# Gates and branch products of a hybrid encoder with tokens on the partitions and 512 weight columns moving

## The chip, the core and the metric

The kernel runs on one core of one Trainium2 chip. The metric is the device time of one execution in microseconds. A profile is one execution recorded by the hardware profiler; its span runs from the first to the last instruction, and the time of that execution is a little longer than its span.

## The reference, cut to what matters

There are two layers, 256 tokens, a width of 1024 and fp32 throughout. A layer mixes the tokens in three ways beside each other (differential attention, a gated DeltaNet, windowed attention), each giving 512 channels. Each branch is multiplied by its own 512 x 1024 matrix and gated by a sigmoid of a projection of x; the three are summed and go through the output projection. A norm and an FFN follow.

```python
z = x @ w_in                                   # ... its last 3 * 1024 columns are gz
ys = jnp.stack([y_a, y_b, y_c], axis=2)        # 256 x 3 x 512
proj = jnp.einsum('btnc,ncd->btnd', ys, w_branch)
gates = jax.nn.sigmoid(gz.reshape(B, T, N_BRANCHES, D))
merged = jnp.sum(gates * proj, axis=2)
return merged @ w_out
```

## The kernel before

Nearly all of the work is fp32 products on TensorE. Each operand is held as a high half, rounded to the format in which TensorE is fast (`F32R`), and a low half, the rest; a product is three matmuls (`mm3`: high by high, high by low, low by high). Weights come in tiles of 128 x 1024 fp32, 512 KB each, packed on the host in the order of `_blocks`. `take` issues the load of a tile on SP's queue, copies it to the high half on ScalarE (`hi_take`) and subtracts to get the low half on VectorE (`lo_take`); there are 4 buffers each of the raw tile and of the two halves, and all weights form one stream in a fixed order.

There are two ways to lay out a projection. With channels on the partitions (`proj_ch`, and `pair` for two blocks of 128 channels in one PSUM bank) a 128 x 128 block of the weight is stationary and the 256 tokens of x^T (`xTh`, `xTl`) move. With tokens on the partitions (`token_major`, and `proj_tok` for the output projection `wo` and the FFN's way down `fd`) a slice of 128 tokens of x^T, or of the tile that holds the branch or FFN output, is stationary and 512 weight columns move.

`merge` returns `product`, which makes one product named in `ORDER`. A gate (`gz`, 12 a layer: 3 branches x 4 groups of 256 channels) is a `pair` followed by a tanh on ScalarE into a tile `g`; the sigmoid is (tanh + 1) / 2, and the half is applied at the end. A branch product (`wb`, 12 a layer) takes one weight tile and 24 matmuls of 256 tokens into one bank; then VectorE computes (g + 1) x product, and adds to the other branches' parts. After the third branch, ScalarE copies the sum, halved, to a high half and VectorE subtracts to get the low half (tiles `z` and `kk`, named `mh` and `ml`). They are then the stationary operand of the output projection, which needs channels on the partitions.

The order in which each engine works is written out before the kernel runs. Python records every operation (`Plan.record`; all of them carry line 195 in the profile), and `Plan.emit` walks through them as a list scheduler with estimated costs, ranks, and the offsets of `PRIO`. `ORDER` sets the order of the weight stream of the mixer's products. PSUM has 8 banks in three groups: 4 `mm` for the projections, 2 `ch` for the DeltaNet, 2 `at` for the attentions; the norm at the end of a part uses `ch` and `at` for its transposes. Gates and branch products that are ready fill TensorE while the mixers wait for other engines.

Of the kernel before, what the change touches and what calls it, by code (L numbers as in the profile page):

```python
# [10 lines left out]
F32 = mybir.dt.float32  # L11
F32R = mybir.dt.float32r
# [3 lines left out]
ALU = mybir.AluOpType  # L16
# [32 lines left out]
PRIO = {(0, 'a', 'ak', 0): -2.6, (0, 'a', 'aq', 1): 1.1, (0, 'a', 0): -0.1, (0, 'a', 1): 8.0, (0, 'a', 2): 6.9, (0, 'a', 3): -2.3, (0, 'ab', 0): -2.2, (0, 'aq', 0): -9.3, (0, 'aq', 1): -4.4, (0, 'c', 'ckv', 0): -20.4, (0, 'c', 'cq', 0): 5.9, (0, 'c', 0): -2.6, (0, 'c', 1): 2.1, (0, 'c', 2): -0.9, (0, 'cq', 0): 5.9, (0, 'cq', 1): 2.3, (0, 'finish'): -6.6, (0, 'gate', 1): 5.2, (0, 'gz', 0): -19.3, (0, 'gz', 1): -1.5, (0, 'gz', 3): -2.8, (0, 'k', 'ab', 0): -1.0, (0, 'k', 'gate', 0): -7.9, (0, 'k', 'gate', 1): 6.1, (0, 'k', 'q', 1): 2.4, (0, 'k', 'v', 0): -2.7, (0, 'k', 'v', 1): 7.3, (0, 'k', 0): -0.9, (0, 'k', 1): -10.1, (0, 'q', 0): 4.4, (0, 'q', 1): 8.0, (0, 'scan'): -3.1, (0, 'v', 0): -0.6, (0, 'v', 1): 4.5, (0, 'wb', 0): 5.9, (0, 'wb', 1): 4.2, (0, 'wb', 2): 4.8, (0, 'wb', 3): -13.0, (0, 'wb', 4): 7.1, (0, 'wb', 5): 4.3, (0, 'wb', 6): 7.1, (0, 'wb', 7): -4.2, (0, 'wb', 8): 0.1, (1, 'a', 'ak', 1): -4.1, (1, 'a', 'aq', 0): -0.2, (1, 'a', 'aq', 1): -4.3, (1, 'a', 0): 0.3, (1, 'a', 1): 3.1, (1, 'a', 3): -0.4, (1, 'ab', 0): -2.2, (1, 'ak', 0): 0.5, (1, 'ak', 1): 1.5, (1, 'aq', 1): 5.7, (1, 'av', 0): 5.4, (1, 'c', 'ckv', 0): 3.0, (1, 'c', 'cq', 0): -2.2, (1, 'c', 0): -3.8, (1, 'c', 1): 1.2, (1, 'ckv', 0): 3.0, (1, 'cq', 0): -1.5, (1, 'finish'): -4.0, (1, 'gate', 0): 7.5, (1, 'gate', 1): -5.5, (1, 'gz', 0): 3.8, (1, 'gz', 10): 4.4, (1, 'gz', 11): -5.4, (1, 'gz', 3): 8.2, (1, 'gz', 4): -3.2, (1, 'gz', 5): 0.4, (1, 'gz', 7): -3.0, (1, 'gz', 8): 14.3, (1, 'gz', 9): -2.7, (1, 'k', 'ab', 0): -3.5, (1, 'k', 'gate', 1): 1.4, (1, 'k', 'k', 0): -0.9, (1, 'k', 'q', 0): 3.4, (1, 'k', 'q', 1): 7.0, (1, 'k', 'v', 0): 3.3, (1, 'k', 'v', 1): 6.9, (1, 'k', 0): 5.2, (1, 'q', 0): 11.6, (1, 'q', 1): 1.6, (1, 'scan'): 0.7, (1, 'solve'): -7.1, (1, 'v', 0): 1.5, (1, 'v', 1): -1.0, (1, 'wb', 0): 8.7, (1, 'wb', 10): 2.6, (1, 'wb', 11): -3.3, (1, 'wb', 2): -2.3, (1, 'wb', 3): 3.1, (1, 'wb', 4): 4.9, (1, 'wb', 5): -1.6, (1, 'wb', 6): 2.9, (1, 'wb', 7): 9.9, (1, 'wb', 8): 3.9, (1, 'wb', 9): -0.1}  # L49
# [4 lines left out]
ORDER = [[('av', 0), ('ab', 0), ('k', 0), ('ak', 0), ('gz', 10), ('aq', 0), ('k', 1), ('q', 0), ('aq', 1), ('q', 1), ('ak', 1), ('gz', 1), ('v', 0), ('v', 1), ('gz', 0), ('gate', 0), ('gate', 1), ('cq', 0), ('wb', 1), ('ckv', 0), ('gz', 11), ('gz', 2), ('gz', 3), ('wb', 0), ('cq', 1), ('wb', 2), ('wb', 3), ('gz', 9), ('wb', 9), ('gz', 4), ('wb', 11), ('gz', 5), ('gz', 6), ('wb', 10), ('gz', 7), ('wb', 4), ('gz', 8), ('wb', 6), ('wb', 7), ('wb', 8), ('wb', 5)], [('av', 0), ('ab', 0), ('k', 0), ('ak', 0), ('gz', 10), ('aq', 0), ('k', 1), ('q', 0), ('aq', 1), ('q', 1), ('ak', 1), ('v', 1), ('gz', 0), ('gz', 3), ('v', 0), ('gate', 0), ('gate', 1), ('ckv', 0), ('gz', 1), ('cq', 0), ('wb', 1), ('wb', 0), ('gz', 11), ('gz', 2), ('cq', 1), ('wb', 2), ('gz', 9), ('wb', 3), ('gz', 4), ('wb', 9), ('wb', 11), ('gz', 5), ('gz', 6), ('wb', 10), ('wb', 4), ('gz', 8), ('gz', 7), ('wb', 6), ('wb', 7), ('wb', 8), ('wb', 5)]]  # L54


SIZES = {F32: 4, F32R: 4, F16: 2, U8: 1}
# [376 lines left out]
def _blocks(depth=DEPTH):  # L434

    out = []

    def cols(key, name, l, c0, n, nk=KD, k0=0, sub=()):
        out.append((key, nk, n, lambda i: i[name][(l,) + sub][k0 * P:(k0 + nk) * P, c0:c0 + n]))

    for l in range(depth):
        for nme, c, m in (("k", 2048, 4), ("q", 1536, 4), ("v", 2560, 4), ("gate", 3072, 4), ("aq", 0, 4), ("ak", 512, 4)):
            for b in range(m):
                cols((nme, l, b), "w_in", l, c + b * P, P)
        for b in range(4):
            cols(("av", l, b), "w_in", l, 1024, 512, 2, b * 2)
        for t in range(4):
            sel = np.concatenate([3600 + g * 256 + t * 64 + np.arange(64) for g in range(2)])
            out.append((("cq", l, t), KD, P, lambda i, l=l, sel=sel: i["w_in"][l][:, sel]))
        for b in range(2):  # L450
            cols(("ckv", l, b), "w_in", l, 4112 + b * P, P)
        for n in (0, 2, 1):
            for m in range(4):
                for b in range(2):
                    cols(("gz", l * 3 + n, 2 * m + b), "w_in", l, 4368 + n * D + (2 * m + b) * P, P)
                if n != 2:
                    cols(("wb", l, n, m), "w_branch", l, m * 256, 256, 4, sub=(n,))
                else:
                    sel = np.concatenate([g * 256 + t * 64 + np.arange(64) for t in range(4) for g in range(2)])
                    out.append((("wb", l, n, m), 4, 256, lambda i, l=l, m=m, sel=sel: i["w_branch"][l, 2][sel, m * 256:(m + 1) * 256]))  # L460
# [12 lines left out]
    return out  # L473
# [21 lines left out]
def tile_encoder_trunk(ctx: ExitStack, tc: tile.TileContext, a: dict, out: bass.AP, depth=DEPTH, tap=None):  # L495
# [191 lines left out]
    def pair(nme, l, b):  # L687
        return proj_ch([(nme, l, 2 * b + c) for c in range(2)])
# [691 lines left out]
    def merge(l, pr, ys, mh, ml):  # L1380
        gates, macc = {}, {}

        def product(nme, b):
            if nme == "av":
                return token_major(nme, l, "q")
            if nme == "ab":
# [8 lines left out]
                return ps  # L1395
            if nme == "gz":
                n, m = divmod(b, 4)
                ps = pair("gz", l * 3 + n, m)
                gates[b] = buf("g", (P, 2, T))
                S.activation(gates[b], ps, AF.Tanh, scale=0.5)  # L1400
                return None
            if nme != "wb":
                return pair(nme, l, b)
            n, m = divmod(b, 4)
            yh, yl = ys[n]
            gt = gates.pop(b)
            hi, lo = take(("wb", l, n, m))
# [20 lines left out]
    for l in range(depth):  # L1428
# [12 lines left out]
        tap(f"merged{l}", mh[0])  # L1441
# [64 lines left out]
```

## Time and profile before

| | |
|---|---|
| median of 3 executions | 993.6 us (992.38 to 994.38) |
| the profiled execution | 992.73 us |
| its span | 991.0 us |
| TensorE matmul busy | 969.0 us, 7598 instructions |
| VectorE, ScalarE, GpSimd busy | 722.3, 588.8, 73.0 us |
| read from HBM | 163.12 MB |

The page cuts the span into 40 equal slices and shows busy shares in tenths. The chain of work that ended last is followed back from the last instruction to what released each step. Busy times of matmuls overlap and their ends are modelled, so the spacing of matmuls is read from stretches of the chain.

### The profile page before, as it was taken

How to read it: one execution, taken by the hardware profiler on the slowest of the kernel's cores; microseconds unless marked ns; L12 is line 12 of the kernel's file. 1: busy time of each engine (PE TensorE's matmuls, PEld its weight loads, DVE VectorE, ACT ScalarE, POOL GpSimd, SP SyncE). 2: the span in 40 equal slices, each digit the busy share in tenths (PEclk: the TensorE clock that was granted, in tenths of full speed). 3: DMA queues.
4: the chain of work that ended last, by engine and by line, in shares of the span. 5: the costliest groups of instructions: out<-in, count | busy, mean ns of one | idle time of the engine just before them, and what ended most of it. 6: DMA issues, size and time to landing. Idle time of an engine off the chain costs nothing.

```text
span 991.0 us, 19154 instructions
## 1 busy us (share of the span) xinstructions
PE 969.0 (98%) x7598; PEld 906.2 (91%) x7598; DVE 722.3 (73%) x1310; ACT 588.8 (59%) x1068; POOL 73.0 (7%) x84
## 2 busy tenths in 40 slices
PE   7999999999999999999999999999999999999996
PEld 6899999989988999988889999999899799999885
DVE  6799786665689766665688996966756995667555
ACT  5868966664455655553557787757744654555441
POOL 0520010100000100000005200000000010000000
PEclk9999999999999999999999999999999999999998
DMA  7644355464575655555635543425445855555661
GB/s 266 187 153 147 102 148 145 144 182 138 178 248 168 203 187 186 172 175 188 213 104 158 165 121 115 146 81 176 154 137 181 273 190 159 191 180 188 196 191 42
DMA packets 50109, 165.43 MB, mean 167 GB/s; under 512 B 5751, under 2 KB 11271, under 8 KB 50020
## 3 DMA queue, kind: packets, MB, share of 16 engines
q1 hardware_dynamic: 48644, 159.78, 50.9%
q0 software_dynamic: 1376, 4.43, 1.5%
q8 instruction: 59, 0.97, 0.4%
q14 instruction: 30, 0.25, 0.1%
HBM read 163.12 MB, written 1.07 MB: 166 GB/s over the span
## 4 chain that ended last, share of the span: by engine, by line
PE 81%; DVE 6%; ACT 4%; DMA 2%; POOL 1%; issue 1%; POOLq 0%; DVEq 0%; ACTq 0%
PE mm_proj_ch L195 48%; PE ch_run L195 6%; PE mm_product L195 6%; PE mm_run L195 6%; PE mm_token_major L195 3%; PE at_window L195 2%; PE at_attention L195 2%; PE ch_solve L195 2%; DMA raw_proj_tok<-in_w_dram 2%; PE ch_gdn L195 1%; ACT hi_take L195 1%; PE ch_scan L195 1%; DMA raw_take<-in_w_dram 1%; PE ch_finish L195 1%; POOL x_decay L195 1%
## 5 line engine op out<-in xcount | busy, mean ns | idle before, releaser
L195 PE MATMUL mm_proj_ch<-xTh,hi_take 128*128 128x256 f32 x1488 | 421.8, 286 | 0.9 <-ACT hi_take L195 0.5
L195 PE MATMUL mm_proj_ch<-xTl,hi_take 128*128 128x256 f32 x1488 | 420.2, 285 | 0.0
L195 PE MATMUL mm_proj_ch<-xTh,lo_take 128*128 128x256 f32 x1488 | 419.1, 285 | 0.0
L195 DVE TENSOR_TENSOR lo_take<-raw_take,hi_take 128x1024 fp32r<-128x1024 f32 x219 | 266.8, 1232 | 104.5 <-ACT hi_take L195 86.4
L195 ACT ACTIVATE hi_take<-raw_take 128x1024 fp32r<-128x1024 f32 x214 | 224.4, 1057 | 195.0 <-PE mm_proj_ch L195 136.5
L195 PEld LDWEIGHTS mm_proj_ch<-xTh,hi_take 128*128 128x128 f32 x1488 | 280.2, 189 | 3.5 <-ACT hi_take L195 1.8
L195 PEld LDWEIGHTS mm_proj_ch<-xTh,lo_take 128*128 128x128 f32 x1488 | 279.5, 189 | 2.8 <-issue 1.6
L195 PEld LDWEIGHTS mm_proj_ch<-xTl,hi_take 128*128 128x128 f32 x1488 | 280.2, 189 | 1.6 <-issue 0.8
L195 ACT ACTIVATE hi_proj_tok<-raw_proj_tok 128x1024 fp32r<-128x1024 f32 x50 | 52.8, 1060 | 66.8 <-PE mm_run L195 37.9
L195 DVE TENSOR_TENSOR lo_proj_tok<-raw_proj_tok,hi_proj_tok 128x1024 fp32r<-128x1024 f32 x50 | 61.0, 1223 | 42.9 <-ACT hi_proj_tok L195 42.9
L195 DVE SCALAR_TENSOR_TENSOR z_conv_silu<-mm_proj_ch,col_params,z_conv_silu 128x254 f32<-128x254 f32 (+1 forms) x96 | 39.1, 474 | 0.6 <-ACT z_conv_silu L195 0.5
L195 DVE SCALAR_TENSOR_TENSOR g_product<-g_product,mm_product 128x512 f32<-128x512 f32 x24 | 16.5, 686 | 24.5 <-PE mm_product L195 24.5
L195 POOL TENSOR_TENSOR s_tail<-s_tail,nhalf 128x1 f32<-128x1 f32 x8 | 5.3, 665 | 380.4 <-DVE s_tail L195 380.4
L195 ACT ACTIVATE e_window<-e_window,s_window 128x256 f32<-128x256 f32 x55 | 26.5, 498 | 10.5 <-DVE s_window L195 10.4
L195 PEld LDWEIGHTS <-h_solve 128*128 128x128 f16 x640 | 25.8, 98 | 4.2 <-ACT h_solve L195 0.4
L195 PE MATMUL mm_run<-hi_proj_tok,tile_encoder_trunk 128*128 128x512 f32 x88 | 27.5, 392 | 1.6 <-ACT tile_encoder_trunk L195 1.2
L195 PE MATMUL mm_run<-hi_proj_tok,ile_encoder_trunk 128*128 128x512 f32 x88 | 27.3, 391 | 0.0
L195 ACT ACTIVATE e_attention<-e_attention,s_attention 128x256 f32<-128x256 f32 x46 | 22.7, 503 | 5.3 <-DVE s_attention L195 5.1
L195 PE MATMUL mm_product<-ya_attention,hi_take 128*128 128x256 f32 x128 | 25.1, 287 | 0.0
L195 PE MATMUL mm_product<-ya_gdn,hi_take 128*128 128x256 f32 x128 | 23.7, 283 | 0.0
L195 PE MATMUL mm_product<-yc_window,hi_take 128*128 128x256 f32 x128 | 23.7, 283 | 0.0
L195 ACT ACTIVATE tile_encoder_trunk<-tile_encoder_trunk 128x512 f32<-128x512 f32 (+1 forms) x22 | 13.6, 625 | 16.6 <-DVE tile_encoder_trunk L195 16.6
(348 smaller groups left out, 1656.0 us busy)
## 6 DMA issues: line engine op xcount, KB each, us to landing
raw_take<-in_w_dram SPq DMA_DIRECT2D x226, 512.0 KB, 4.2
raw_proj_tok<-in_w_dram SPq DMA_DIRECT2D x60, 512.0 KB, 4.0
G_load_G<-band SPq DMA_DIRECT2D x24, 192.0 KB, 3.5
ya_ln_params<-in_lnp_dram POOLq DMA_DIRECT2D x16, 256.0 KB, 5.9
x<-in_xT_dram SPq DMA_DIRECT2D x4, 256.0 KB, 4.5
x<-in_x_dram SPq DMA_DIRECT2D x2, 512.0 KB, 4.6
out_dram<-x SPq DMA_DIRECT2D x8, 128.0 KB, 1.8
_tile_encoder_trunk<-in_w_dram SPq DMA_DIRECT2D x4, 128.0 KB, 3.7
```

What stands on the lines that cost most here:

```text
L195: op.ways.append((eng, lambda fn=fn, args=args, kw=kw: fn(*args, **kw), _cost(eng, name, outs, ins, args, kw), table))
```

## The change

`product` no longer uses `pair` for the gates, nor 256 moving tokens for the branch products. Both are made 512 channels at a time: the slice of 128 tokens of x^T (gates) or of the branch's output (branch products) is stationary, and 512 columns of the weight move, into two PSUM banks, one for each half of the tokens. A gate is 4 weight tiles, a branch product is 2; there are 6 of each in a layer. Gating and summing are as before, on tiles with tokens on the partitions. The sum of the three branches is then turned over by four transposes on TensorE into a bank of the group `at`, and the copy to the high half and the subtraction read that bank. The output projection finds its stationary slices at the new places. `_blocks` packs the weights accordingly. `ORDER` and `PRIO` name the new products, and have other values for the rest too.

```diff
-ORDER = [[('av', 0), ('ab', 0), ('k', 0), ('ak', 0), ('gz', 10), ('aq', 0), ('k', 1), ('q', 0), ('aq', 1), ('q', 1), ('ak', 1), ('gz', 1), ('v', 0), ('v', 1), ('gz', 0), ('gate', 0), ('gate', 1), ('cq', 0), ('wb', 1), ('ckv', 0), ('gz', 11), ('gz', 2), ('gz', 3), ('wb', 0), ('cq', 1), ('wb', 2), ('wb', 3), ('gz', 9), ('wb', 9), ('gz', 4), ('wb', 11), ('gz', 5), ('gz', 6), ('wb', 10), ('gz', 7), ('wb', 4), ('gz', 8), ('wb', 6), ('wb', 7), ('wb', 8), ('wb', 5)],
...
+ORDER = [[('av', 0), ('ab', 0), ('k', 0), ('ak', 0), ('aq', 0), ('k', 1), ('gz', 0), ('q', 0), ('aq', 1), ('q', 1), ('ak', 1), ('v', 0), ('v', 1), ('gz', 1), ('gate', 0), ('gate', 1), ('cq', 0), ('ckv', 0), ('wb', 0), ('cq', 1), ('wb', 1), ('gz', 4), ('gz', 5), ('wb', 4), ('gz', 2), ('wb', 5), ('gz', 3), ('wb', 2), ('wb', 3)],
...
         for n in (0, 2, 1):
-            for m in range(4):
+            for h in range(2):
+                for b in range(KD // 2):
+                    cols(("gz", l * 3 + n, h, b), "w_in", l, 4368 + n * D + h * 512, 512, 2, b * 2)
                 for b in range(2):
-                    cols(("gz", l * 3 + n, 2 * m + b), "w_in", l, 4368 + n * D + (2 * m + b) * P, P)
-                if n != 2:
-                    cols(("wb", l, n, m), "w_branch", l, m * 256, 256, 4, sub=(n,))
...
+                    if n != 2:
+                        cols(("wb", l * 3 + n, h, b), "w_branch", l, h * 512, 512, 2, b * 2, sub=(n,))
...
+            if nme not in ("gz", "wb"):
+                return pair(nme, l, b)
+
+            n, h = divmod(b, 2)
+            nk = KD if nme == "gz" else 4
+            pss = [ps_mm() for _ in range(2)]
+            for c in range(nk // 2):
+                w = take((nme, l * 3 + n, h, c if nme == "gz" else 1 - c))
+                for tt in range(2):
+                    ts = slice(tt * P, (tt + 1) * P)
+                    for j in range(2):
+                        if nme == "gz":
+                            lh, ll = xTh[:, 2 * c + j, ts], xTl[:, 2 * c + j, ts]
+                        else:
+                            lh, ll = [y[1 - c][:, j, ts] for y in ys[n]]
+                        mm3(pss[tt], lh, ll, w[0][j], w[1][j], c == j == 0, 2 * c + j == nk - 1)
             if nme == "gz":
-                n, m = divmod(b, 4)
-                ps = pair("gz", l * 3 + n, m)
-                gates[b] = buf("g", (P, 2, T))
-                S.activation(gates[b], ps, AF.Tanh, scale=0.5)
+                gates[b] = [buf("g") for _ in range(2)]
+                for tt in range(2):
+                    S.activation(gates[b][tt], pss[tt], AF.Tanh, scale=0.5)
                 return None
...
-            ps = ps_mm((P, 2, T))
-            for c in range(2):
-                cs = slice(c * P, (c + 1) * P)
-                for j in (3, 2, 1, 0):
-                    mm3(ps[:, c], hi[j][:, cs], lo[j][:, cs], yh[j // 2][:, j % 2], yl[j // 2][:, j % 2], j == 3, j == 0)
-            V.scalar_tensor_tensor(gt, gt, 1.0, ps, ALU.add, ALU.mult)
-            parts = macc.setdefault(m, [])
-            parts.append(gt)
-            if len(parts) > 1:
-                V.tensor_tensor(parts[0], parts[0], gt, op=ALU.add)
-            if len(parts) == 3:
-                h_, l_ = [buf(("z", "kk")[m // 2], (P, 2, T), F32R) for _ in range(2)]
-                S.activation(h_, parts[0], AF.Copy, scale=0.5)
-                V.scalar_tensor_tensor(l_, parts[0], 0.5, h_.bitcast(F32), ALU.mult, ALU.subtract)
-                mh[m], ml[m] = h_, l_
+            for tt, gt in enumerate(gates.pop(b)):
+                V.scalar_tensor_tensor(gt, gt, 1.0, pss[tt], ALU.add, ALU.mult)
+                parts = macc.setdefault((h, tt), [])
+                parts.append(gt)
+                if len(parts) > 1:
+                    V.tensor_tensor(parts[0], parts[0], gt, op=ALU.add)
+                if len(parts) == 3:
+                    ps = ps_at((P, 4, P))
+                    for k in range(4):
+                        TE.transpose(ps[:, k], parts[0][:, k * P:(k + 1) * P], ident)
+                    h_, l_ = [buf(("z", "kk")[h], (P, 4, P), F32R) for _ in range(2)]
+                    S.activation(h_, ps, AF.Copy, scale=0.5)
+                    V.scalar_tensor_tensor(l_, ps, 0.5, h_.bitcast(F32), ALU.mult, ALU.subtract)
+                    mh[h, tt], ml[h, tt] = h_, l_
...
-        lhs = lambda k, tt: (mh[k // 2][:, k % 2, tt * P:(tt + 1) * P], ml[k // 2][:, k % 2, tt * P:(tt + 1) * P])
+        lhs = lambda k, tt: (mh[k // 4, tt][:, k % 4], ml[k // 4, tt][:, k % 4])
```

## Rows read from the trace of the kernel before

**Rows 1.** The page: busy time by engine, and busy tenths in 40 slices.
```profile
PE 969.0 (98%) x7598; PEld 906.2 (91%) x7598; DVE 722.3 (73%) x1310; ACT 588.8 (59%) x1068; POOL 73.0 (7%) x84
...
PE   7999999999999999999999999999999999999996
...
PEclk9999999999999999999999999999999999999998
```

**Rows 2.** Waits of TensorE (us in total, times, longest): first and last of 14.
```profile
PE mm_proj_ch L195 <- ACT _tile_encoder_trunk L195: 5.5, 1, 5.5
PE mm_run L195 <- ACT tile_encoder_trunk L195: 1.2, 1, 1.2
PE mm_token_major L195 <- DVE xTl L195: 0.9, 2, 0.5
...
PE mm_proj_ch L195 <- ACT q_token_major L195: 0.2, 1, 0.2
```

**Rows 3.** The chain in order of time: start us, us, what.
```profile
234.81 5.51 PE mm_product L195 x46
...
341.08 92.17 PE mm_proj_ch L195 x768
...
794.05 5.12 PE mm_token_major L195 x22
...
921.94 29.95 PE mm_run L195 x132
```

**Rows 4.** The chain at two runs of transposes; TensorE's timeline around four others.
```profile
201.16 0.87 PE ch_finish L195 x8
...
579.07 1.79 PE ch_gdn L195 x16
...
308.83 0.38 PE L195 MATMUL ch_tail<-tri,q_tail 128*128 128x128 f32 x2
309.05 0.38 PE L195 MATMUL at_tail<-tri,q_tail 128*128 128x128 f32 x2
309.19 0.48 PE L195 MATMUL mm_token_major<-yc_weights,xTh 128*128 128x512 f32 x1
309.50 0.39 PE L195 MATMUL mm_token_major<-yc_weights,xTl 128*128 128x512 f32 x1
```

**Rows 5.** Instructions on the tiles g and kk: ns min/median/max, first and last start.
```profile
L195 ACT ACTIVATE g_product<-mm_proj_ch x24: 573/579/609, 95.9 to 771.0; 128x512 f32<-128x512 f32 x24
L195 DVE SCALAR_TENSOR_TENSOR g_product<-g_product,mm_product x24: 681/686/689, 188.3 to 772.3; 128x512 f32<-128x512 f32 x24
L195 DVE TENSOR_TENSOR g_product<-g_product,g_product x16: 685/692/693, 239.3 to 773.0; 128x512 f32<-128x512 f32 x16
L195 ACT ACTIVATE kk_product<-g_product x4: 615/624/636, 267.5 to 774.0; 128x512 fp32r<-128x512 f32 x4
L195 DVE SCALAR_TENSOR_TENSOR kk_product<-g_product,kk_product x4: 684/686/693, 269.3 to 775.2; 128x512 fp32r<-128x512 f32 x4
```

**Rows 6.** DMA issues: count, KB each, median us to landing.
```profile
raw_take<-in_w_dram SPq DMA_DIRECT2D x226, 512.0 KB, 4.2
```

**Rows 7.** The chain in the windowed attention and at layer 0's handover.
```profile
212.25 1.08 ACT e_window L195 x5
...
274.27 0.70 DVE g_product L195
...
275.60 2.05 DVE lo_proj_tok L195 x2
...
279.19 1.22 DVE lo_proj_tok L195
...
283.38 7.56 DMA raw_proj_tok<-in_w_dram
```

**Rows 8.** VectorE's steps of the convolutions: ns min/median/max, first and last start.
```profile
L195 DVE SCALAR_TENSOR_TENSOR z_conv_silu<-mm_proj_ch,col_params,z_conv_silu x96: 465/474/484, 16.5 to 619.9; 128x254 f32<-128x254 f32 x48, 128x255 f32<-128x255 f32 x48
```

**Rows 9.** Busy us of PE, PEld, DVE, ACT, POOL in a stretch; clock; DMA share.
```profile
60.00:120.00 60.00, 59.50 (x697) 57.15 (x696) 53.28 (x112) 51.34 (x112) 6.39 (x7) 1.00 0.37 115
```

More of the change, by code (lines that the diff above doesn't have):

```diff
@@ L53 @@
 KEEP = {'wo': (4, ('D', 'N', 'x')), 'fd': ((4, ('g', 'g')), (4, ('g', 'g')))}
-ORDER = [[('av', 0), ('ab', 0), ('k', 0), ('ak', 0), ('gz', 10), ('aq', 0), ('k', 1), ('q', 0), ('aq', 1), ('q', 1), ('ak', 1), ('gz', 1), ('v', 0), ('v', 1), ('gz', 0), ('gate', 0), ('gate', 1), ('cq', 0), ('wb', 1), ('ckv', 0), ('gz', 11), ('gz', 2), ('gz', 3), ('wb', 0), ('cq', 1), ('wb', 2), ('wb', 3), ('gz', 9), ('wb', 9), ('gz', 4), ('wb', 11), ('gz', 5), ('gz', 6), ('wb', 10), ('gz', 7), ('wb', 4), ('gz', 8), ('wb', 6), ('wb', 7), ('wb', 8), ('wb', 5)], [('av', 0), ('ab', 0), ('k', 0), ('ak', 0), ('gz', 10), ('aq', 0), ('k', 1), ('q', 0), ('aq', 1), ('q', 1), ('ak', 1), ('v', 1), ('gz', 0), ('gz', 3), ('v', 0), ('gate', 0), ('gate', 1), ('ckv', 0), ('gz', 1), ('cq', 0), ('wb', 1), ('wb', 0), ('gz', 11), ('gz', 2), ('cq', 1), ('wb', 2), ('gz', 9), ('wb', 3), ('gz', 4), ('wb', 9), ('wb', 11), ('gz', 5), ('gz', 6), ('wb', 10), ('wb', 4), ('gz', 8), ('gz', 7), ('wb', 6), ('wb', 7), ('wb', 8), ('wb', 5)]]
+ORDER = [[('av', 0), ('ab', 0), ('k', 0), ('ak', 0), ('aq', 0), ('k', 1), ('gz', 0), ('q', 0), ('aq', 1), ('q', 1), ('ak', 1), ('v', 0), ('v', 1), ('gz', 1), ('gate', 0), ('gate', 1), ('cq', 0), ('ckv', 0), ('wb', 0), ('cq', 1), ('wb', 1), ('gz', 4), ('gz', 5), ('wb', 4), ('gz', 2), ('wb', 5), ('gz', 3), ('wb', 2), ('wb', 3)], [('av', 0), ('ab', 0), ('k', 0), ('ak', 0), ('aq', 0), ('k', 1), ('gz', 0), ('q', 0), ('aq', 1), ('q', 1), ('ak', 1), ('v', 0), ('v', 1), ('gz', 1), ('gate', 0), ('gate', 1), ('cq', 0), ('ckv', 0), ('wb', 0), ('cq', 1), ('wb', 1), ('gz', 4), ('gz', 5), ('wb', 4), ('gz', 2), ('wb', 5), ('gz', 3), ('wb', 2), ('wb', 3)]]
 SIZES = {F32: 4, F32R: 4, F16: 2, U8: 1}
@@ L452, in _blocks @@
         for n in (0, 2, 1):
-            for m in range(4):
+            for h in range(2):
+                for b in range(KD // 2):
+                    cols(("gz", l * 3 + n, h, b), "w_in", l, 4368 + n * D + h * 512, 512, 2, b * 2)
                 for b in range(2):
-                    cols(("gz", l * 3 + n, 2 * m + b), "w_in", l, 4368 + n * D + (2 * m + b) * P, P)
-                if n != 2:
-                    cols(("wb", l, n, m), "w_branch", l, m * 256, 256, 4, sub=(n,))
-                else:
-                    sel = np.concatenate([g * 256 + t * 64 + np.arange(64) for t in range(4) for g in range(2)])
-                    out.append((("wb", l, n, m), 4, 256, lambda i, l=l, m=m, sel=sel: i["w_branch"][l, 2][sel, m * 256:(m + 1) * 256]))
+                    if n != 2:
+                        cols(("wb", l * 3 + n, h, b), "w_branch", l, h * 512, 512, 2, b * 2, sub=(n,))
+                    else:
+                        sel = np.concatenate([g * 256 + t * 64 + np.arange(64) for t in (2 * b, 2 * b + 1) for g in range(2)])
+                        out.append((("wb", l * 3 + n, h, b), 2, 512, lambda i, l=l, h=h, sel=sel: i["w_branch"][l, 2][sel, h * 512:(h + 1) * 512]))
         for half in range(2):
@@ L1395, in product @@
                 return ps
+            if nme not in ("gz", "wb"):
[10 more added lines that the diff above has]
+                            lh, ll = xTh[:, 2 * c + j, ts], xTl[:, 2 * c + j, ts]
+                        else:
+                            lh, ll = [y[1 - c][:, j, ts] for y in ys[n]]
+                        mm3(pss[tt], lh, ll, w[0][j], w[1][j], c == j == 0, 2 * c + j == nk - 1)
@@ L1396, in product @@
             if nme == "gz":
-                n, m = divmod(b, 4)
-                ps = pair("gz", l * 3 + n, m)
-                gates[b] = buf("g", (P, 2, T))
-                S.activation(gates[b], ps, AF.Tanh, scale=0.5)
-                return None
[L1402 to L1407, printed above, removed]
-            ps = ps_mm((P, 2, T))
-            for c in range(2):
-                cs = slice(c * P, (c + 1) * P)
-                for j in (3, 2, 1, 0):
-                    mm3(ps[:, c], hi[j][:, cs], lo[j][:, cs], yh[j // 2][:, j % 2], yl[j // 2][:, j % 2], j == 3, j == 0)
@@ L1440, in tile_encoder_trunk @@
                 late.append((SY.dma_start(out=x[:, tt], in_=a["x"][0, tt * P:(tt + 1) * P]), 50 + 2 * tt))
-        tap(f"merged{l}", mh[0])
         norm = Norm(l, 1, pr["ln1_g"], pr["ln1_b"], False)
-        lhs = lambda k, tt: (mh[k // 2][:, k % 2, tt * P:(tt + 1) * P], ml[k // 2][:, k % 2, tt * P:(tt + 1) * P])
+        lhs = lambda k, tt: (mh[k // 4, tt][:, k % 4], ml[k // 4, tt][:, k % 4])
         proj_tok("wo", l, KD, lhs, norm)
```

2 lines of the change are left out of this document (1 added, 1 removed).

## The prediction

> **What bounds the kernel now.** I read the page's busy times first, then what TensorE waited for, then the chain of work that ended last in order of time, then the rows of the tiles that the diff touches. The reader is to see that TensorE is the bound nearly everywhere and that it is not slowed from outside: it is busy for 969.0 of 991.0 us, at a granted clock of 2.4 GHz, 0.9 or more of full speed, until the last slice [rows 1]. A busy TensorE is not a full one, since matmul ends are modelled, so the waits come next: in the whole span it stood with a named releaser for 11.8 us in 14 entries, 5.5 of them before the first matmul, and no entry names a PSUM bank that a reader had not yet emptied [rows 2]. So time that the change takes off TensorE should be nearly time off the end, and time that it adds to TensorE nearly time added.
>
> The price of a matmul is not the duration that the profile gives it, since matmuls overlap, but the spacing in a stretch where nothing else runs. The chain gives such stretches. With 256 moving columns: 768 in 92.17 us, 0.1200 us each, for x moving past stationary weights, and 46 in 5.51 us, 0.1198, for the branch products. With 512 moving columns there are two prices: 132 in 29.95 us, 0.2269, where the stationary operand is a slice of a mixer or FFN tile, and 22 in 5.12 us, 0.2327, where it is a slice of x^T [rows 3]. Two matmuls of 256 columns cost 0.240, so a matmul of 512 saves 0.013 or 0.007 us per pair. The gain per pair is small, and which price applies decides half of the gain.
>
> **The gates.** Before: 12 pairs a layer, each 2 blocks x 8 row blocks x 3 matmuls of 256 columns, so 576 a layer and 1152 in all: 1152 x 0.1200 = 138.2 us. After: 6 products a layer, each 4 weight tiles x 2 token halves x 2 x 3 matmuls of 512 columns, so 576 in all. Their stationary operand is xTh or xTl and their moving one is a weight tile, which is word for word the form of the token-major row: 576 x 0.2327 = 134.0, a gain of 4.2. By the other price 576 x 0.2269 = 130.7, a gain of 7.5. I take 4.2, because the operands are those of that row, and keep 7.5 as the other end.
>
> **The branch products.** Before 12 x 24 x 2 = 576 matmuls of 256: 576 x 0.1198 = 69.0 us. After 288 of 512 columns, stationary a slice of a mixer's output tile, so nearest to the 0.2269 row: 65.3, a gain of 3.7. By the dearer price 67.0, a gain of 2.0.
>
> **The turning over.** It is new: 4 transposes for each of 2 column halves x 2 token halves x 2 layers, 32 in all. Transposes in a row cost 0.87 us for 8 and 1.79 us for 16, so 0.109 to 0.112 each [rows 4]: 32 x 0.112 = 3.6 us. Beside that, a matmul of 512 columns that follows transposes starts its successor late: the one at 309.19 is followed after 0.31 us instead of 0.23 [rows 4]. Once for each of the 8 groups that is 0.6 us; nothing at the other end, if the planner puts groups together.
>
> **What is moved or stays equal.** The tanh (24 of 579 ns), the gating (24 of 686), the sums (16 of 692), the copies to the high half (8 of about 624) and the subtractions (8 of about 686) keep count and size, all 128x512 [rows 5]. The copy and the subtraction now read PSUM; ScalarE's 579 ns from PSUM against 624 from SBUF says that this is not dearer, and VectorE's 686 is the same from either [rows 5]. Weight tiles stay 72 of 512 KB over both layers, one copy and one subtraction each, on the same queue [rows 6]; a gate's tile now lasts TensorE 12 x 0.2327 = 2.8 us instead of 24 x 0.120 = 2.9, so no transfer has to be faster by more than a few per cent. No transfer is moved past another kind: the weights stay one stream on SP in a new order, and POOL's loads of the norm parameters still wait for the same freed tiles. What hides the equal work is TensorE's own stream; without that cover a group's sum, copy and subtraction cost 2.0 us.
>
> **The new waits.** First, a transpose waits for VectorE's sum, and behind it in TensorE's fixed order stand the output projection's matmuls. Before, the finished half went from VectorE to ScalarE directly. The handover already ran close: the chain leaves TensorE at 274.27 for VectorE's gating and the subtractions of the output weights, and then for a transfer of 7.56 us [rows 7]. TensorE had other matmuls meanwhile. After the last product the first column half needs no waiting, and its matmuls with two weight tiles and both token halves are 2 x 12 x 0.2269 = 5.4 us of cover; one group's path is 0.69 + 0.69 + 4 x 0.112 + 0.58 + 0.69 = 3.1 us, and the second group's VectorE work adds 2.1: 5.2 us. It just fits, so I cost it at nothing. Without the cover it is what stands in VectorE's queue ahead, two subtractions of weights of 1.2 us each [rows 7], 2.4 us a layer.
>
> Second, a gate holds two PSUM banks of four for 48 x 0.2327 = 11.2 us, where a pair held one for 48 x 0.120 = 5.8. Behind it in the first part of a layer stand the convolved projections, whose banks VectorE empties in 2 x 4 x 0.474 = 3.8 us each [rows 8], with VectorE at 53.28 of 60 us there [rows 9]. Two free banks and 11.2 us of gate matmuls to hide 3.8 us: at nothing, unless VectorE is more than 7.4 us behind.
>
> **The sum.** -4.2 - 3.7 + 3.6 + 0.6 = -3.7 us. The cheap ends give -7.5 - 3.7 + 3.6 = -7.6; the dear ends -4.2 - 2.0 + 4.2 = -2.0. The profiled execution took 992.73 us (span 991.0), so 989.0 by its own time; the median shown is 0.9 above it, so on that scale 989.9, with 986.0 to 991.6 as this case's own range.
>
> One rule speaks against the change. The Trainium skill, "TensorE: Matmul & The Clock Gate", section "Back-to-back issue gap", gives columns at one per cycle of 2.4 GHz and some 2.5 ns for each matmul. By that, 864 matmuls fewer are an estimate of 2.2 us, its 55.8 ns for 128 columns make 32 transposes 1.8 us, and the change would be worth under half a microsecond. The trace doesn't agree: the page's 109 ns for 256 columns stand here at 120, its 216 for 512 at 227 [rows 3].
>
> **The rivals.** (a) Not faster, because a gate's two banks starve the projections. For it: VectorE's load early in a layer [rows 9]. Against it: no bank wait among the 14 entries [rows 2]. Four gates stand among the convolutions (two a layer); if two of them leave TensorE waiting for one emptying of 3.8 us, +7.6: 997.5. It decides from one full emptying on, which eats the whole 3.7. (b) The handover takes the gain: 2.4 us in each of two layers, +4.9 on the sum, 994.8, within 991 to 997. For it: VectorE and the transfer are on the chain there [rows 7]. Against: the cover computed above. (c) No gain per column: a matmul of 512 columns costs two of 256 when its moving operand is a fresh weight tile; then only the turning over is left, +4.2, 997.8. The token-major row, which moves fresh weights, speaks against it at 0.2327 against 0.240. (d) More than the sum: all at 0.2269, and the new order, which puts 5.4 us of branch product and two gates of 11.2 us between the last projection of the windowed attention and its product, fills the stretch in which its softmax on ScalarE and VectorE is on the chain from 212.25 [rows 7]; about 2 us a layer more than -7.6 would give 982 to 986, taken as 984.
>
> **How the numbers follow.** Chances: the sum 0.57, (a) 0.13, (b) 0.17, (c) 0.04, (d) 0.09. A difference of 0.2% is 2.0 us, about what a measurement of this kernel can tell from none. Faster: 0.51 from the sum and all of (d), 0.60. Same: 0.06 from the sum, 0.12 from (b) and 0.01 from (a), 0.19. Slower: 0.21, the rest. The predicted time is the sum's, 989.9. From 984 to 999 the range leaves out half of (d) and somewhat over half of (a), about 0.12, with the rest of the 0.2 for what I didn't think of.
>
> **What would show it.** Right: the gate's matmuls spaced 0.232 to 0.233 us, the branch products' 0.227, 32 transposes at 0.11, TensorE's waits still near 12 us. (a) would show as waits of projections for VectorE's convolutions or as wide spacing right behind a gate; (b) as a wait of transposes or of the output projection on VectorE near 275 and 765 us; (c) as spacing of 0.240; (d) as both forms at 0.227 and a mixer stage shorter by more than its matmuls. The prediction is wrong if TensorE's gaps between products, which the list of waits hardly shows, change by more than 4 us with the new order.

## The result and the profile after

| | before | after |
|---|---|---|
| median | 993.87 us (992.38 to 994.38) | 985.95 us (985.11 to 986.52) |
| ratio | | 0.9924, interval 0.9911 to 0.9938 |
| profiled execution, its span | 992.73, 991.0 us | 986.52, 984.8 us |
| TensorE instructions | 7598 | 6766 |

The kernel became faster by 7.9 us by the medians, 6.2 by the spans of the two profiles. The forecast was 3.7 us faster; the time lies inside the range of 984 to 999, just below the sum's own range of 986.0 to 991.6.

The page of the changed kernel: busy time by engine and busy tenths, to be held against [rows 1].

```profile
PE 960.6 (98%) x6766; PEld 859.9 (87%) x6766; DVE 724.2 (74%) x1313; ACT 586.9 (60%) x1065; POOL 72.5 (7%) x84
...
PE   7999999999999999999999999999999999999996
...
PEclk9999999999999999999999999999999999999999
```

TensorE is busy 8.4 us less and still bounds the kernel. What it waited for (us in total, times, longest), to be held against [rows 2]: four of the first eight, and the last, of 15.

```profile
PE mm_proj_ch L195 <- ACT _tile_encoder_trunk L195: 5.1, 2, 4.9
PE ch_tail L195 <- DVE q_tail L195: 1.5, 1, 1.5
PE mm_run L195 <- ACT ile_encoder_trunk L195: 1.2, 1, 1.2
...
PE mm_product L195 <- DVE z_conv_silu L195: 0.5, 1, 0.5
...
PE at_window L195 <- DVE yc_window L195: 0.2, 1, 0.2
```

All 15 come to 14.4 us, 2.6 more than before. None is a transpose of the sum, and none an output projection (`mm_run`) that waits for `z` or `kk`; the `mm_run` here belongs to the FFN's way down, as in [rows 2]. One is a PSUM bank of the projections: at 540.45 a gate's matmul, which doesn't read `z_conv_silu`, starts right behind the last convolution step with which VectorE reads a bank. Read in the same way, `at_window` behind `yc_window` is a bank of the group `at`, and so is the last entry of [rows 2] one of the group `mm`: a matmul behind the ScalarE copy that empties a bank. All of these are short, 0.2 to 0.5 us.

The chain of the changed kernel in order of time, at the long products of both layers and a windowed softmax ahead of those of layer 1, their handover to the output projection in layer 0, and the start of the FFN and of the way down; to be held against [rows 3] and [rows 7].

```profile
208.78 62.52 PE mm_product L195 x269
271.30 0.44 PE at_product L195 x4
271.74 1.39 PE mm_product L195 x6
273.13 0.44 PE at_product L195 x4
273.56 5.50 PE mm_product L195 x24
279.06 1.82 PE mm_run L195 x8
280.87 0.44 PE at_product L195 x4
281.31 1.40 PE mm_run L195 x6
...
339.70 91.86 PE mm_proj_ch L195 x768
...
435.26 29.31 PE mm_run L195 x128
...
704.08 1.26 ACT e_window L195 x5
...
713.71 44.02 PE mm_product L195 x190
...
916.43 29.32 PE mm_run L195 x128
```

The gates, mixed with some branch products, are spaced 62.52 / 269 = 0.2324 and 44.02 / 190 = 0.2317; the last branch product is spaced 5.50 / 24 = 0.229. From 271 to 282 the chain passes through the transposes and never leaves TensorE. Before, it ran there over VectorE and a transfer of 7.56 us [rows 7].

TensorE's timeline around two groups of transposes in layer 1:

```profile
757.57 0.60 PE L195 MATMUL at_product<-tri,g_product 128*128 128x128 f32 x4
757.93 0.48 PE L195 MATMUL mm_product<-hi_take,ya_gdn 128*128 128x512 f32 x1
758.24 0.60 PE L195 MATMUL at_product<-tri,g_product 128*128 128x128 f32 x4
758.60 0.48 PE L195 MATMUL mm_product<-hi_take,ya_gdn 128*128 128x512 f32 x1
758.91 0.40 PE L195 MATMUL mm_product<-lo_take,ya_gdn 128*128 128x512 f32 x1
```

Four transposes take 0.36 us, and the matmul behind them is followed after 0.31 us instead of 0.23: 0.36 + 0.08 = 0.44. That is the chain's 0.44 for a group, so the slowed step behind the group was already in the chain's 0.11 for each transpose [rows 4], and the forecast's extra 0.6 us counted it twice.

The other engines' instructions on the changed tiles (ns minimum, median, maximum; first and last start), to be held against [rows 5]:

```profile
L195 ACT ACTIVATE g_product<-mm_product x24: 572/598/667, 135.0 to 750.5; 128x512 f32<-128x512 f32 x24
...
L195 DVE SCALAR_TENSOR_TENSOR g_product<-g_product,mm_product x24: 679/681/689, 199.2 to 762.4; 128x512 f32<-128x512 f32 x24
...
L195 ACT ACTIVATE kk_product<-at_product x4: 578/599/601, 281.4 to 767.6; 128x512 fp32r<-128x512 f32 x4
```

They kept count and size, as forecast, and the copies of the sum to the high half, now from PSUM, take 596 (`z`) and 599 ns (`kk`) by the median where those from SBUF took 624.

**Where the 6.2 us went.** TensorE's timeline can be cut into steps from each matmul's start to the next one's, and the steps summed by product; idle time then counts to the product ahead of it. The gates of before carry the same name as other channel projections; they are taken as what those projections shrink by, 576 matmuls a layer, as if the others had not changed.

| us of TensorE's timeline | before | after | difference | forecast |
|---|---|---|---|---|
| gates and branch products, layer 0 | 109.2 | 106.2 | -3.0 | -3.95 |
| gates and branch products, layer 1 | 110.1 | 104.2 | -5.9 | -3.95 |
| transposes | 0 | 2.8 | +2.8 | +4.2 |
| all else (from the span) | | | -0.1 | 0 |
| span | 991.0 | 984.8 | -6.2 | -3.7 |

The prices come from the chain of the kernel before, at its own gates and branch products in layer 0, and, for comparison, at the FFN of layer 1:

```profile
257.10 4.63 PE mm_proj_ch L195 x39
...
263.03 2.63 PE mm_product L195 x22
...
893.21 28.30 PE mm_proj_ch L195 x238
```

A gate's matmul of 256 columns was spaced 4.63 / 39 = 0.1187 us (0.1188 over all gates from 237 to 275 us), not the 0.1200 of the FFN's long stretch in layer 0 [rows 3]; the FFN of layer 1 has 0.1189. A branch product's was 2.63 / 22 = 0.1195. After the change the two are 0.2324 and 0.229. So the gates' matmuls gained 1152 x 0.1188 - 576 x 0.2324 = 3.0 us and the branch products' 576 x 0.1195 - 288 x 0.229 = 2.9.

At these prices a layer's gates and branch products would take 102.8 us before and 99.9 after. The rest, 6.4 and 7.3 us before, 6.3 and 4.3 after, is time beyond the prices; it hardly moved in layer 0 and fell by 3.0 in layer 1. Not all of it is TensorE standing still. Of the 864 matmuls in the changed kernel's products, 67 come right behind a matmul of another kind (transposes, attention, DeltaNet) and have a step that is 0.04 to 0.12 us longer, like the 0.31 above; together these are 5.8 of the 10.6 us. The end of the way down's long run of matmuls, a mark that nothing overtakes, agrees: 466.3 before and 464.6 after in layer 0, 951.9 and 945.8 in layer 1, so 1.7 us came from layer 0 and 4.4 from layer 1.

### The profile page after: what moved, and what is told of

Same layout as the page of the kernel before. It is cut to its first block, busy times and chain, and to the rows that moved or that the text cites. A ratio compares the mean times of both kernels' runs of the same rounds, so it can differ in the third digit from the quotient of the medians.

```text
span 984.8 us, 17469 instructions
## 1 busy us (share of the span) xinstructions
PE 960.6 (98%) x6766; PEld 859.9 (87%) x6766; DVE 724.2 (74%) x1313; ACT 586.9 (60%) x1065; POOL 72.5 (7%) x84
## 4 chain that ended last, share of the span: by engine, by line
PE 83%; ACT 7%; DVE 6%; DMA 1%; issue 1%; POOL 1%; SPq 0%; POOLq 0%; ACTq 0%; DVEq 0%
PE mm_proj_ch L195 37%; PE mm_product L195 17%; PE mm_run L195 8%; PE ch_run L195 8%; PE mm_token_major L195 4%; PE ch_solve L195 2%; PE at_attention L195 2%; ACT e_window L195 2%; ACT hi_take L195 1%; DVE lo_take L195 1%; PE at_window L195 1%; DVE z_conv_silu L195 1%; PE ch_gdn L195 1%; POOL D_decay L195 1%; ACT s_window L195 1%
## 5 line engine op out<-in xcount | busy, mean ns | idle before, releaser
L195 PE MATMUL mm_proj_ch<-xTh,hi_take 128*128 128x256 f32 x1104 | 310.6, 285 | 0.7 <-ACT hi_take L195 0.6
L195 PE MATMUL mm_proj_ch<-xTh,lo_take 128*128 128x256 f32 x1104 | 309.7, 284 | 0.0
L195 PE MATMUL mm_proj_ch<-xTl,hi_take 128*128 128x256 f32 x1104 | 309.4, 283 | 0.0
L195 PEld LDWEIGHTS mm_proj_ch<-xTh,hi_take 128*128 128x128 f32 x1104 | 207.6, 189 | 2.4 <-ACT hi_take L195 0.8
L195 PEld LDWEIGHTS mm_proj_ch<-xTl,hi_take 128*128 128x128 f32 x1104 | 207.8, 189 | 0.7 <-DVE xTl L195 0.2
L195 PEld LDWEIGHTS mm_proj_ch<-xTh,lo_take 128*128 128x128 f32 x1104 | 207.3, 189 | 1.0 <-DVE lo_take L195 0.4
L195 PE MATMUL mm_product<-hi_take,xTh 128*128 128x512 f32 x192 | 76.7, 406 | 1.0 <-DVE z_conv_silu L195 0.5
L195 PE MATMUL mm_product<-lo_take,xTh 128*128 128x512 f32 x192 | 76.9, 402 | 0.1
L195 PE MATMUL mm_product<-hi_take,xTl 128*128 128x512 f32 x192 | 76.4, 399 | 0.0
L195 PEld LDWEIGHTS mm_product<-lo_take,xTh 128*128 128x128 f32 x192 | 36.3, 189 | 7.8 <-DVE lo_take L195 0.8
```

What stands on the lines that cost most here:

```text
L195: op.ways.append((eng, lambda fn=fn, args=args, kw=kw: fn(*args, **kw), _cost(eng, name, outs, ins, args, kw), table))
```

## The experiments

The first theory was that the two layout terms (-7.9) come through whole and that the transposes cost nothing, since they stand in a handover where TensorE waits anyway. Its rival was that the layout is worth the forecast's 3.7 us and the rest is the new order of work. e1, e2 and e4 to e6 change what is issued with the order of work held; e3 and e7 to e12 change the order. Changes against the changed kernel are differences of medians to 985.95; e1 to e4, e5 to e8 and e9 to e12 had the kernel before beside them at 992.47, 992.71 and 992.78 us. The diffs are shortened to what they do.

**e1: the moving operand halved again.** 768 of the 864 gate and branch matmuls are issued as two of 256 columns.

```diff
-mm3(pss[tt], lh, ll, w[0][j], w[1][j], c == j == 0, 2 * c + j == nk - 1)
+# each of mm3's matmuls but those with start or stop:
+for c0 in (0, 256):
+    nc.tensor.matmul(ps[:, c0:c0 + 256], lx, rx[:, c0:c0 + 256], start=start, stop=stop)
```

> The changed kernel with the same order on every engine, but 768 of the 864 gate and branch matmuls are issued as two of 256 moving columns (the first and the last of each bank stay whole). Theory P (the price per column is what the layout gains): 528 gate matmuls cost 0.240 instead of 0.2324 and 240 branch matmuls 0.239 instead of 0.2267, so +4.0 + 3.0 = +7.0 us on the changed kernel, about 993. Theory L (the layout gains by something else, and the moving width is not the cause): within 1 us of the changed kernel, about 986.

Measured 989.12 us (987.29 to 991.88), ratio 0.9969 [0.9958, 0.998]: 3.2 us slower than the changed kernel. In TensorE's timeline the products took 215.0 us instead of 210.3, so the halving cost 4.6 us there, less than twice the 0.1200 of [rows 3] would have made (7.0) and near what twice 0.1188 and 0.1195 makes (528 x 0.0052 + 240 x 0.010 = 5.1); 3.2 of them reached the end. The gain from 512 columns is real, and a matmul of 512 does not cost two of 256.

**e2: no turning over.** The transposes are left out; the copy and the subtraction read the sum as it is, so the output projection gets operands with rows and columns exchanged.

```diff
-TE.transpose(ps[:, k], parts[0][:, k * P:(k + 1) * P], ident)
+# nothing is issued in its place
-S.activation(h_, ps, AF.Copy, scale=0.5)
+S.activation(h_, parts[0], AF.Copy, scale=0.5)
```

> The changed kernel with the same order, without the 32 transposes: the copy and the subtraction read the sum before it is turned over, so the output projection multiplies a wrong operand and only the turning over is left out. Theory P: every transpose is on TensorE's path, -3.6 - 0.6 = -4.2 us on the changed kernel, about 981.8. Theory L (TensorE has slack there, the handover is bound by VectorE or by transfers): 0 to -1 us.

Measured 988.1 us (985.32 to 989.35), ratio 0.9948 [0.9933, 0.9963]: no faster than with the transposes. Two stretches at half the clock lie in its profile, of which more below; at 1.6 us each, as an estimate, its span without them would be 984.5, against 984.8. In layer 0 the last product's last matmul does start earlier, at 277.1 instead of 278.7, but the output projection's last one only 0.7 us earlier. The chain of this kernel shows why:

```profile
274.25 1.23 DVE lo_proj_tok L195
...
275.49 7.54 DMA raw_proj_tok<-in_w_dram
...
283.60 1.05 ACT hi_proj_tok L195
```

With TensorE's transposes gone, the transfer of the output projection's weights sets the handover again, as before the change [rows 7]; in layer 1 too, with 5.25 us. By these two profiles taking 3.5 us of transposes out is worth 0.3 us. Two profiles of equal work differ by more (982.3 us in e4), so what is shown is that no gain near 3.5 us came.

**e5 and e6: work added with the order held.** e5 issues every transpose twice; e6, the control, issues the first matmul of each of the 24 gate groups twice.

```diff
 # e5
-TE.transpose(ps[:, k], parts[0][:, k * P:(k + 1) * P], ident)
+plan.record(("PE", "transpose", twice(nc.tensor.transpose), (ps[:, k], parts[0][:, k * P:(k + 1) * P], ident), {}))
 # e6
+if nme == "gz" and c == j == 0:
+    plan.record(("PE", "matmul", twice(nc.tensor.matmul), (pss[tt], lh, w[0][j]), {"start": True, "stop": False}))
...
```

> The changed kernel with each of the 32 transposes issued twice, in the same order of work; the output stays the same. If the transposes stand in stretches in which TensorE waits for VectorE or for weights anyway (hidden), 32 more cost 0 to 1 us against the changed kernel, ratio to the kernel before 0.992 to 0.9935. If they stand on the work that sets the end (paid), 32 x 0.09 to 0.112 = 2.9 to 3.6 us more, ratio 0.9953 to 0.996.

> The control: the changed kernel with the first of the 24 matmuls of each of the 24 gate groups issued twice (the first time into a closed group, so the output stays the same), in the same order of work: 24 x 0.2325 = 5.6 us of TensorE's time in the gates. If TensorE sets the time in the stretches with gates, 4 to 5.6 us more than the changed kernel, ratio to the kernel before 0.9965 to 0.998. If the mixer stage has slack that takes up such additions, as the halved matmuls let suppose, 0 to 3 us more, ratio 0.9924 to 0.9955.

e5 measured 988.52 us (986.7 to 990.47), ratio 0.9948 [0.9931, 0.9966]: 2.6 us slower for 32 x 0.108 = 3.5 us more on TensorE. e6 measured 989.8 us (988.24 to 991.4), ratio 0.9965 [0.9951, 0.9978]: 3.9 us slower for 5.6. So about 0.7 of what is added to TensorE reaches the end, in the gates and in the transposes alike. The share depends on what is taken as the changed kernel's time: by the ratios to the kernel before beside each, e1, e5 and e6 are 4.5, 2.4 and 4.1 us slower, which is between 0.7 and all of what was added. That is against the first theory: the transposes are not free, they are just at the edge, where the handover is as long by TensorE as by the transfer. Less of them gains nothing that shows, more of them costs.

**e3: the kernel before in the new order.** ORDER and PRIO of the changed kernel, each product of 512 channels written as its two of 256.

```diff
-ORDER = [[('av', 0), ('ab', 0), ('k', 0), ('ak', 0), ('gz', 10), ('aq', 0), ('k', 1), ('q', 0),
+ORDER = [[('av', 0), ('ab', 0), ('k', 0), ('ak', 0), ('aq', 0), ('k', 1), ('gz', 0), ('gz', 1), ('q', 0),
...
```

> The kernel before, layout untouched, with the changed kernel's order of weights and planner offsets (each product of 512 channels replaced by its two products of 256 in a row, with its offset). Theory P (layout gives -3.7, the other 4 of the -7.9 come from the new order and offsets): 989 to 991. Theory L (all of it comes from the layout): 993 to 996, the old time or worse, since the offsets were made for other products.

Measured 1001.64 us (1000.19 to 1003.17), ratio 1.009 [1.0076, 1.0104]: slower by 9.2 us. The new order by itself gives the old layout nothing; it was made for the other one, which is 15.7 us faster in it. The reverse, the changed kernel in the order of before, was not run.

**e7 to e12: three pairs of the two layouts under other offsets.** In each kernel PRIO alone is changed: emptied, halved, or layer 1 given the values of layer 0.

```diff
+PRIO = {}                                          # e7 after, e8 before
+PRIO = {k: v / 2 for k, v in PRIO.items()}         # e9 after, e10 before
+PRIO = {(l,) + k[1:]: v for l in (0, 1) for k, v in PRIO.items() if k[0] == 0}   # e11 after, e12 before
```

> The changed kernel with the table of offsets PRIO emptied; ORDER stays. To be read against e8, the kernel before with its table emptied. If the gain comes from the layout alone (gates -4.2, branch products -3.7, transposes hidden), this one is 7 to 8 us faster than e8. If the layout is worth the 3.7 us of the forecast and the tuned offsets the rest, 3 to 4 us faster than e8. Both are expected slower than with their tables, by 5 to 30 us.

> The kernel before with the table of offsets PRIO emptied; ORDER stays. Layout alone: 7 to 8 us slower than e7. Layout 3.7 and offsets the rest: 3 to 4 us slower than e7. Whatever the difference is beyond 8 us would be the planner's luck with either order.

> The changed kernel with every offset of PRIO halved; ORDER stays. To be read against e10, the kernel before with its offsets halved. With all offsets (profiles) the layout with its own order gained 1.7 us in the mixer of layer 0 and 6.1 in that of layer 1; with none, e7 was 2.8 us faster than e8. If the layout by itself is worth 7 us and more, this one is 6 to 9 us faster than e10, and both layers gain alike. If the layout is worth the 3 to 4 us of its matmuls and transposes, and the rest is stalls of TensorE that one order has and another has not, the pair differs by 0 to 6 us, and the two layers differ from each other by several us, not in the same way as in the tuned pair.

> The kernel before with every offset of PRIO halved; ORDER stays. Layout worth 7 us by itself: 6 to 9 us slower than e9. Layout worth 3 to 4 us and the rest the order's stalls: 0 to 6 us slower than e9. Both are expected above their tuned kernels, by 5 to 25 us.

> The changed kernel with layer 1 given the offsets of layer 0 (ORDER is the same for both of its layers already). Layer 0 should stay as it was, output projection ending near 296 us. If the layout by itself gains 6 us in layer 1's mixer, it ends that mixer 5 to 7 us sooner than e12 by stage length. If those 6 us are the order's, the stage lengths of layer 1 differ by another amount, 0 to 4 us or with the other sign.

> The kernel before with layer 1 given the offsets of layer 0; the two ORDER lists stay. Layer 0 as before, output projection ending near 298 us. Layout worth 6 us in layer 1: its mixer stage takes 5 to 7 us longer than in e11. The order's: another difference, 0 to 4 us or with the other sign.

| offsets | before's layout | new layout | difference | layer 0, layer 1 (profiles) |
|---|---|---|---|---|
| tuned | 993.87 | 985.95 | -7.9 | -1.7, -4.4 |
| none (e8, e7) | 1018.85 | 1016.04 | -2.8 | -4.0, +2.1 |
| halved (e10, e9) | 1016.93 | 1002.0 | -14.9 | -10.8, -4.2 |
| layer 0's in both (e12, e11) | 1011.23 | 997.45 | -13.8 | -2.2, -13.0 |

The last column is the mark at the end of the way down's long run. Their ratios to the kernel before: e7 1.0226 [1.0207, 1.0245], e8 1.0256 [1.0235, 1.0277], e9 1.0087 [1.0074, 1.0101], e10 1.0246 [1.0232, 1.0261], e11 1.0042 [1.0026, 1.0057], e12 1.0189 [1.0172, 1.0205]. The new layout is faster in all four pairs, but by 2.8 to 14.9 us, and layer by layer between 13.0 us faster and 2.1 slower, where the operations are the same and only their order differs. Layer 0 of the last pair has the offsets of the tuned kernels and repeats their difference (-2.2 against -1.7), so this scatter belongs to the orders and not to the measurement.

By the estimate below, most of the scatter is the clock. In e7 to e12 TensorE's granted clock falls from 2.4 to 1.2 GHz for a while, behind places where the order has left it thinly used. Here are, for e7 and then for e8, the 3 us ahead of such a stretch at the handover of layer 0, and all stretches at half the clock. Columns: stretch; its length, busy us (count) of PE, PEld, DVE, ACT, POOL; granted clock, DMA share, GB/s.

```profile
190.50:197.30 6.80, 5.95 (x16) 4.40 (x17) 4.28 (x21) 5.39 (x18) 0.00 (x0) 0.50 0.27 57
...
286.50:289.50 3.00, 1.22 (x4) 0.59 (x4) 3.00 (x5) 2.07 (x5) 0.10 (x1) 1.00 0.92 298
289.50:296.30 6.80, 5.81 (x18) 4.86 (x19) 5.99 (x10) 4.62 (x9) 0.00 (x0) 0.50 0.90 299
...
685.40:695.60 10.20, 7.36 (x30) 6.00 (x30) 6.16 (x32) 7.84 (x25) 1.67 (x2) 0.50 0.22 56
...
791.30:794.70 3.40, 3.40 (x12) 2.71 (x11) 2.96 (x5) 2.55 (x5) 0.00 (x0) 0.51 0.90 301
```

```profile
74.00:77.40 3.40, 3.31 (x29) 3.13 (x30) 3.35 (x6) 3.24 (x5) 0.00 (x0) 0.50 0.62 202
...
217.40:220.80 3.40, 3.40 (x15) 2.26 (x16) 0.98 (x4) 1.47 (x4) 0.00 (x0) 0.50 0.00 0
...
292.90:295.90 3.00, 1.20 (x4) 0.67 (x4) 3.00 (x5) 3.00 (x6) 0.53 (x1) 1.00 0.98 300
295.90:299.30 3.40, 3.10 (x7) 2.48 (x8) 2.05 (x4) 0.03 (x1) 0.00 (x0) 0.50 0.94 306
...
794.20:797.60 3.40, 3.40 (x10) 2.64 (x9) 1.28 (x3) 0.00 (x0) 0.00 (x0) 0.51 0.99 383
```

The tuned kernels have no such stretch before their last matmuls. On the way down one of 3.4 us cost 1.6 us (see the last section), so half of the length is an estimate of what a stretch costs, on the high side where TensorE also stands within it.

| offsets | us at half the clock, before's layout | new layout | difference of the spans | less the clock's part, an estimate |
|---|---|---|---|---|
| tuned | 0 | 0 | -6.2 | -6.2 |
| none | 13.7 | 27.3 | -2.0 | -8.8 |
| halved | 17.1 | 3.4 | -15.0 | -8.2 |
| layer 0's in both | 17.1 | 6.8 | -15.2 | -10.1 |

All executions of these kernels bear it out: the mean granted clock is 0.984 in e7 and 0.989 to 0.993 in e8, 0.993 to 0.996 in e9 and 0.986 to 0.989 in e10. Without the clock's part the new layout gains 6 to 10 us in every pair, and in each layer of every pair (1.7 to 7.9). By the prices above and 0.44 us for each of the 8 groups it would be -3.0 - 2.9 + 3.5 = -2.4, in any order. What goes beyond, some 4 us in the tuned pair and 6 to 8 in the others, is time beyond the prices, which the new layout had less of each time; 0.6 to 0.9 us of it lies ahead of the first matmul. Neither theory as written holds: the layout's own price is not 7 us, and the pairs differ by more than 0 to 6, by way of the clock.

Without offsets, the handover that the forecast feared does come. What TensorE waited for in e7:

```profile
PE mm_run L195 <- DVE z_product L195: 4.3, 2, 2.2
...
PE mm_run L195 <- ACT z_product L195: 1.5, 2, 0.8
```

and in e8, the kernel before without offsets:

```profile
PE mm_run L195 <- DVE z_product L195: 3.3, 2, 1.6
PE mm_run L195 <- ACT z_product L195: 3.2, 2, 1.6
```

There all eight transposes of the first column half follow the last product in a row, and TensorE stands 5.8 us, over both layers, for the output projection's operands. But the layout of before stands 6.5 us at the same place, so it is no price of the turning over alone. In both kernels the clock falls right behind it (289.5 and 791.3 in e7, 295.9 and 794.2 in e8).

**e4: the address of x^T.** 96 bytes are allocated ahead of `xTh`, to see whether its place is why a matmul with x^T stationary costs more than one with a mixer's tile.

```diff
+cp.tile([P, 24], F32, name="pad")
 xTh = cp.tile([P, KD, T], F32R, name="xTh")
```

> The changed kernel with 96 bytes in front of the x^T tiles, so that they and everything behind them start elsewhere (x^T at a multiple of 4096 bytes, the rest at a multiple of 64). If the gate's dearer price of 0.2324 against 0.2267 hangs on where x^T lies: gates at about 0.227, -3.3 us for the gates and -1.1 for the token-major projections, about 981.5. If it hangs on something else of these operands: 0.2324 as before and about 986.

Measured 985.15 us (983.98 to 986.24), ratio 0.9924 [0.9911, 0.9937], with the gates still spaced 62.55 / 269 = 0.2325. The address is not the cause. As the computation is unchanged, this is also a second measurement of the change: 7.3 us against its own runs of the kernel before.

## Why the prediction was right, and where its size was off

- **The bound.** Right: of time added to TensorE 0.7 or more reaches the end (e1, e5, e6).
- **The gates, -4.2, and the branch products, -3.7: right in kind, too large.** The price for 512 columns holds in the gates, 0.2317 to 0.2324 against the 0.2327 assumed. The one for 256 was taken from the FFN's 768 matmuls at 0.1200, while the gates of before were spaced 0.1187, so the term is -3.0. The branch products came to 0.229 instead of 0.2269, so theirs is -2.9. In the timeline the two terms make -8.9 us, 3.0 more than these prices, all of it less time beyond the prices in layer 1.
- **The turning over, +3.6 and +0.6: counted twice in part.** Each group cost 0.44 us, as priced, but the 0.6 for the matmul behind a group was in that price already. In the timeline the transposes took 2.8 us and the slowed steps behind them the rest, within the products. With this and the terms above the forecast's own sum is -3.0 - 2.9 + 3.5 = -2.4 us, smaller than it stated. And leaving the transposes out gave no gain that shows (e2), because the transfer of the output weights takes the handover over.
- **The new waits, at nothing.** Right for the handover: the first two groups are turned over before the last product ends, the other two lie under matmuls with the first half, and no output projection waits. Nearly right for the banks: a gate waits once, 0.5 us, for a bank that VectorE reads. The reading that no entry of [rows 2] names a bank was not quite right either: the last line there is one, of 0.2 us. Neither changes the sum.
- **The new order, left at nothing.** This is the step that the pairs show to be unsafe. Time beyond the prices is hardly a part of the list of waits, depends on the order, and with the clock that falls in its wake moves by several microseconds a layer for the same operations. The forecast named the gaps as what would make it wrong from 4 us on, and the clock not at all; in the tuned pair the time beyond the prices in gates and branch products moved by 3 us, and neither kernel lost clock in its profile. So more of the gain came from here than from the terms that were forecast, and that the time still fell inside the range is luck, since nothing in the forecast bounded this part: with other offsets the same two layouts differ by 2.8 to 14.9 us.
- **The rivals.** (a), starved projections: refuted by the list of waits, in which no projection waits for VectorE's convolutions and one gate does, for 0.5 us, where (a) priced 3.8 for one emptying. (b), the handover: not in this order; e7 shows its waits, with e8 showing them without the change as well. (c), no gain per column: refuted by the spacing and by e1. (d), more than the sum: its size came nearer than the sum's, but not by its mechanism. The gates are not at 0.2269. The mixer of layer 1 did gain more than its matmuls, as (d) says (5.9 us in the products, 3.0 by price), that of layer 0 did not, and the windowed softmax that (d) wanted covered is on the chain in the changed kernel too (ScalarE's `e_window`, 1.26 us at 704.08).
- **The rule that spoke against.** The Trainium skill, "TensorE: Matmul & The Clock Gate", section "Back-to-back issue gap", would have made the change worth under half a microsecond, as an estimate, by its 2.5 ns for each matmul. The trace after doesn't agree: two of a gate's matmuls of 256 columns took 0.2376 us, one of 512 takes 0.2324, twice the saving of 2.5 ns, and the branch products saved four times as much.

The spans' 6.2 and the medians' 7.9 are apart by what single executions scatter; those at a mean granted clock of 0.998 alone took 992.3 us before (median of 11) and 985.4 after (of 3), 6.9 apart. The layout's own price, -2.4 us, is shown by the spacings, by e1 and by e5; the clock's part in the other pairs is an estimate. What stays open: why the new layout, with the clock's part taken off, had less time beyond the prices in four pairs of four, by some 4 to 8 us. It may be the layout's doing, or each of its orders may have been the better one.

## What to carry to other kernels

Count a change of layout on the bounding engine by the spacing of its instructions in dense stretches, in the stretch that will change and not in a longer one elsewhere (0.1187 against 0.1200 was 1.2 us of this sum), and look whether the duration read from the chain already holds the slowed step behind it before adding that step again. Where the order of work is tuned together with the layout, compare both layouts under several orders before trusting a difference of a few microseconds, and read the granted clock of each first: the same pair gave 2.8 to 14.9 us here, and 6 to 10 in the profiles once the clock's part was taken off. To learn what an operation is worth where two resources end nearly together, both take it out and double it; one of the two alone (no gain that shows, 2.6 us) gives half of the answer.

## What was unexpected of the hardware

**The stationary operand has a price.** With the same kind of moving operand, a weight tile of 512 columns, matmuls with x^T stationary are spaced 0.2324 us and those with a mixer's or FFN's tile 0.2269 to 0.229 ([rows 3], and the chain above). Moving x^T in memory by 96 bytes changed nothing (e4). It is not x^T alone: in the changed kernel's timeline the attention's branch products of layer 0 step by 0.232 us too (median), those of layer 1 and of the other two mixers by 0.227 to 0.228. The cause is open.

**The clock drops where TensorE thins out.** In e2 the granted clock falls to 1.2 GHz, half of its level, for some 3 us, twice: right behind the handover of layer 0 and at the start of the way down. The columns are those of e7 and e8 above.

```profile
296.00:299.00 3.00, 1.45 (x7) 0.87 (x5) 1.44 (x4) 2.12 (x2) 0.57 (x1) 1.00 0.89 289
...
301.00:302.50 1.50, 1.50 (x7) 1.32 (x7) 1.50 (x3) 1.33 (x4) 0.00 (x0) 0.50 0.57 229
```

In the stretch ahead TensorE was busy for 1.45 of 3.00 us. Before's row for the same place has it busy 3.00 of 3.00 at full clock:

```profile
297.00:300.00 3.00, 3.00 (x15) 2.50 (x14) 2.67 (x7) 1.36 (x2) 0.56 (x1) 1.00 0.95 313
```

The price is read at the way down, the same 128 matmuls: 30.93 us in e2's chain where the chain above gives 29.31, so 1.6 us for a drop. The executions of e2 had mean granted clocks of 0.994 to 0.997, those of the changed kernel 0.996 to 0.998. Such drops are a part of the scatter of one to two microseconds between executions, and e2 had more of them, with its thinner handover. In orders that leave TensorE thinner still they come in every execution and cost far more: by the estimate above 13.7 us in e7, 6.8 in e8, 8.5 in e10 and in e12.
